# Shift and scale in units of four k-tiles, their column sums by transposes, in a hybrid decoder layer

## The chip, the cores and the metric

The kernel runs on one core of a Trainium2 chip. The metric is the device time of one execution in microseconds; a lower time is better. TensorE (PE) multiplies matrices, VectorE (DVE) and ScalarE (ACT) work on tiles, SyncE (SP) issues all transfers from HBM; each engine runs its own queue in order, and waits on semaphores for the others.

## What is computed

One decoder layer for 256 tokens of width 4096, in fp32. The part that matters here is the adaptive norm ahead of the first projection:

```python
c_act = jax.nn.silu(c)
mod = c_act @ w_ada[l] + b_ada[l]              # (1, 4096) @ (4096, 3 * 4096)
shift, scale, gate = jnp.split(mod, 3, axis=-1)
h = rmsnorm(x, norm_gain[l])
h = h * (1.0 + scale[:, None, :]) + shift[:, None, :]
proj = jnp.einsum('bsd,dn->bsn', h, w_in[l])   # (256, 4096) @ (4096, 12288)
```

Behind it come sixteen attention heads and four pooling groups on the 24 blocks of 512 columns of `proj`, their gating, the product with `w_out` (4096 x 4096), the factor `gate` with the residual, and a last rmsnorm.

## The kernel before

**Products.** The width of 4096 is cut into 32 k-tiles of 128. `proj` is cut into 24 chunks of 512 columns, which `order` lists. Each fp32 operand is split into a rounded high part and the rest; a product takes three matmuls of 512 columns (high x high, high x low, low x high), for two row tiles of tokens. `split_piece` brings two k-tiles of one chunk (512 KB into a `raw` tile, 7 buffers), lets ACT cast them to `wh` (L237) and DVE take the difference `wl` (L238), 3 buffers each; `products` (L248) issues the 12 matmuls: eight on `wh`, then four on `wl`.

**Visits.** The activations `h` of a k-tile exist only once its shift and scale are summed over all 4096 rows of `w_ada`. The kernel doesn't wait for all of them. It goes round the 24 chunks again and again (L372 to L381), and each `visit` multiplies the chunk by the k-tiles that have become ready since its last visit, in an accumulator `mm` (2 buffers). A chunk's first visit ends with a copy by ACT (L289), each later one with an addition to `accs` by DVE (L291), which here is called its eviction.

**Units.** Shift and scale are made in units of k-tiles (`UNITS`, two each, sixteen in all). `ada_tasks` cuts a unit into tasks of one `raw` tile: 1024 columns of fp32, which are two row blocks of `w_ada` times 2 x 256 columns, in two transfers of 256 KB with rows of 1 KB. `ada_acc` multiplies each block by its column of silu(c) and adds it to `aacc` (128 x 512) with one DVE instruction (L161; the first is L159). `ada_hook` runs after every piece: it adds `2 * RATES[built]` to a credit and runs one task for every 1.456 (`ADA_COST`) of it. With the last task of a unit `build_h` sums `aacc` over its 128 partitions, adds bias and gain (`s12`), and makes the high and low parts `hh` and `hl` of `h` for its k-tiles (ACT L221 and L223, DVE L224). The unit counts as ready two hooks later (`LAG`). The first unit is made ahead of all visits. When all 32 k-tiles are ready the last round of visits runs, with the attention and pooling work, the gate's own additions (`gacc`) and `w_out` behind it.

**Order.** The instructions of each engine stand in an order that the framework's scheduler has fixed when the kernel is built; a tile's number in an order below tells its instance.

In `build_h` before, the sum over partitions is a matmul of each block with a column of ones:

```python
for j in range(2 * uk):
    nc.tensor.matmul(pc[:, j:j + 1], lhsT=acc[:, j * P:(j + 1) * P], rhs=ones, start=True, stop=True)
```

## Time and profile before

| | us |
|---|---|
| median of 3 runs (1558.37 to 1562.53) | 1560.77 |
| profiled execution | 1562.59 |
| its span, first to last instruction | 1560.8 |
| PE busy (7043 instructions) | 1513.5 (97%) |
| DVE busy (1766) | 1409.9 (90%) |
| ACT busy (830) | 703.6 (45%) |

The kernel moves 491 MB, at a mean of 315 GB/s. A matmul that is busy need not be at its peak, since matmuls overlap; the distance from one start to the next is the better measure. Times in the rows are counted from the span's start.

### The profile page before, as it was taken

What the parts mean: (1) busy time and instruction counts of PE and PEld (TensorE: products, weight loads), DVE (VectorE), ACT (ScalarE), POOL (GpSimd) and SP (SyncE); (2) the same over time, 40 slices, a digit from 0 to 9 for tenths busy, and PEclk for the clock granted to TensorE, in tenths of its full rate; (3) what the DMA queues carried; (4) which work ended last, traced back from release to release, by engine and by line L of the source; (5) the groups of instructions that cost most, each with busy time, mean ns of one, the idle gap of its engine ahead of it and who ended that gap; (6) DMA issues with size and microseconds to landing.
All of it is one profiled execution on the core that took longest, in us unless ns stands there. A gap on an engine that the chain in (4) does not pass through costs nothing.

```text
span 1560.8 us, 20366 instructions
## 1 busy us (share of the span) xinstructions
PE 1513.5 (97%) x7043; PEld 1259.0 (81%) x7043; DVE 1409.9 (90%) x1766; ACT 703.6 (45%) x830; POOL 0.7 (0%) x5
## 2 busy tenths in 40 slices
PE   2999999999999999999999999999999999999997
PEld 2877888888888888888888888888898888888875
DVE  5888999999999999899999998999988889988886
ACT  5655343443443434344344344566654444444444
POOL 0000000000000000000000000000000000000000
PEclk9999999999999999999999999999999999999999
DMA  9999999999999999999999998977678999998886
GB/s 330 348 337 356 320 330 324 321 314 338 319 318 328 309 330 310 309 314 328 350 342 324 332 330 305 319 259 231 212 247 269 308 329 358 348 321 325 324 313 258
DMA packets 324087, 491.11 MB, mean 315 GB/s; under 512 B 19320, under 2 KB 150664, under 8 KB 323984
## 3 DMA queue, kind: packets, MB, share of 16 engines
q1 hardware_dynamic: 323984, 489.82, 92.6%
q8 instruction: 55, 0.90, 0.2%
q14 instruction: 48, 0.39, 0.1%
HBM read 485.55 MB, written 4.19 MB: 314 GB/s over the span
## 4 chain that ended last, share of the span: by engine, by line
PE 88%; DVE 4%; DMA 4%; issue 2%; ACT 1%; SPq 1%; DVEq 0%; ACTq 0%
PE mm L248 80%; DMA raw<-in_w_ada_dram 3%; DVE aacc L161 2%; DVE wl L238 1%; PE psm L618 1%; PE psm L248 1%; PE psm L208 1%; PE psm L524 0%; PE psm L523 0%; PE psm L522 0%; DMA raw<-in_w_in_dram 0%; DMA sb<-in_x_dram 0%; PE psm L435 0%; DMA raw<-in_w_out_dram 0%; ACT wh L237 0%
## 5 line engine op out<-in xcount | busy, mean ns | idle before, releaser
L237 ACT CAST wh<-raw 128x1024 fp32r<-128x1024 f32 x514 | 538.4, 1050 | 688.4 <-PE mm L248 547.4
L238 DVE TENSOR_TENSOR wl<-raw,wh 128x1024 fp32r<-128x1024 f32 x514 | 624.5, 1218 | 33.6 <-ACT wh L237 31.6
L248 PE MATMUL mm<-wh,hh 128*128 128x512 f32 x1536 | 604.4, 393 | 5.4 <-ACT wh L237 4.3
L248 PE MATMUL mm<-wh,hl 128*128 128x512 f32 x1536 | 600.1, 391 | 0.0
L248 PE MATMUL mm<-wl,hh 128*128 128x512 f32 x1536 | 414.2, 391 | 0.7 <-DVE wl L238 0.6
L161 DVE SCALAR_TENSOR_TENSOR aacc<-raw,cact,aacc 128x512 f32<-128x512 f32 x496 | 370.9, 748 | 30.2 <-DMA raw<-in_w_ada_dram 22.7
L248 PEld LDWEIGHTS mm<-wh,hh 128*128 128x128 f32 x1536 | 288.8, 188 | 66.8 <-ACT wh L237 7.3
L248 PEld LDWEIGHTS mm<-wl,hh 128*128 128x128 f32 x1536 | 288.4, 188 | 61.3 <-DVE wl L238 1.6
L248 PEld LDWEIGHTS mm<-wh,hl 128*128 128x128 f32 x1536 | 288.9, 188 | 58.2
L248 PE MATMUL mm<-wh,sa 128*128 128x512 f32 x896 | 221.7, 389 | 0.0
L161 DVE SCALAR_TENSOR_TENSOR gacc<-raw,cact,gacc 128x512 f32<-128x512 f32 x248 | 185.6, 748 | 24.9 <-DMA raw<-in_w_ada_dram 21.2
L248 PEld LDWEIGHTS mm<-wh,sa 128*128 128x128 f32 x896 | 168.0, 188 | 34.9
L248 PE MATMUL mm<-wl,sa 128*128 128x512 f32 x448 | 119.8, 389 | 0.0
L291 DVE TENSOR_TENSOR sa<-mm,sa 128x1024 f32<-128x1024 f32 x92 | 112.1, 1218 | 8.6 <-PE mm L248 8.4
L248 PEld LDWEIGHTS mm<-wl,sa 128*128 128x128 f32 x448 | 84.0, 188 | 17.6 <-DVE wl L238 0.2
L291 DVE TENSOR_TENSOR sb<-mm,sb 128x1024 f32<-128x1024 f32 x48 | 58.5, 1219 | 7.3 <-PE mm L248 7.3
L328 PE MATMUL psm<-diag_r,sb 128*128 128x128 f32 x128 | 17.8, 310 | 15.6 <-DVE diag_r L320 15.6
L328 PEld LDWEIGHTS psm<-diag_r,sb 128*128 128x128 f32 x128 | 17.5, 225 | 15.8 <-DVE diag_r L320 15.8
L221 ACT ACTIVATE hf<-xT,s 128x256 f32<-128x256 f32 x32 | 17.5, 594 | 26.0 <-DVE s L213 26.0
L289 ACT COPY sa<-mm 128x1024 f32<-128x1024 f32 x16 | 16.3, 1016 | 15.1 <-PE mm L248 15.1
L672 ACT ACTIVATE yo<-sb 128x512 f32<-128x512 f32 x16 | 10.0, 626 | 25.0 <-DVE sb L670 25.0
L248 PE MATMUL psm<-wh,sa 128*128 128x512 f32 x80 | 20.1, 393 | 0.6 <-ACT wh L237 0.6
(118 smaller groups left out, 632.7 us busy)
## 6 DMA issues: line engine op xcount, KB each, us to landing
raw<-in_w_in_dram SPq DMA_DIRECT2D x384, 512.0 KB, 5.6
raw<-in_w_ada_dram SPq DMA_DIRECT2D x512, 256.0 KB, 5.4
raw<-in_w_ada_dram SPq DMA_DIRECT2D x128, 512.0 KB, 6.0
raw<-in_w_out_dram SPq DMA_DIRECT2D x128, 512.0 KB, 6.4
sb<-in_x_dram SPq DMA_DIRECT2D x16, 512.0 KB, 6.0
raw<-in_w_pool_dram SPq DMA_DIRECT2D x8, 512.0 KB, 4.4
out_dram<-sb SPq DMA_DIRECT2D x16, 256.0 KB, 2.6
fg<-in_final_gain_dram SPq DMA_DIRECT2D x8, 256.0 KB, 4.7
```

Of the source, the lines that this page charges most:

```text
L161: nc.vector.scalar_tensor_tensor(out=acc, in0=r, scalar=cact[:, kt:kt + 1], in1=init if kt == 0 else acc, op0=ALU.mult, op1=ALU.add)
L208: nc.tensor.matmul(pc[:, j:j + 1], lhsT=acc[:, j * P:(j + 1) * P], rhs=ones, start=True, stop=True)
L221: nc.scalar.activation(out=hf[:, i], in_=xT[:, kk + i], func=AF.Identity, scale=s12[:, 1, a + i:a + i + 1], bias=s12[:, 0, a + i:a + i + 1])
L237: nc.scalar.copy(out=wh[:, 0:n], in_=v[:, 0:n])
L238: nc.vector.tensor_tensor(out=wl[:, 0:n], in0=v[:, 0:n], in1=wh[:, 0:n].bitcast(F32), op=ALU.subtract)
L248: nc.tensor.matmul(pt[t], lhsT=hv[i][p][:, t * P:(t + 1) * P], rhs=w[:, i], start=started, stop=ended)
L289: nc.scalar.copy(out=accs[ch], in_=pt)
L291: nc.vector.tensor_tensor(out=accs[ch], in0=pt, in1=accs[ch], op=ALU.add)
L328: nc.tensor.matmul(px[:, i * S + t * P:i * S + (t + 1) * P], lhsT=xs[q][:, t, (2 * a + i) * P:(2 * a + i + 1) * P], rhs=diag_r[:, t], star ...
L618: nc.tensor.matmul(pt[t], lhsT=h[:, t * P:(t + 1) * P], rhs=w, start=False, stop=last and e == len(seq) - 1)
L672: nc.scalar.activation(out=y[:, t], in_=xc[:, t], func=AF.Square, accum_out=ss2[:, t, n:n + 1])
```

## The change

From the third unit on a unit has four k-tiles: `UNITS` is (2, 2, 4, 4, 4, 4, 4, 4, 4). A `raw` tile then holds one row block times 2 x 512 columns, one transfer of 512 KB with rows of 2 KB, and one DVE instruction adds 1024 columns. A unit of four has 32 tasks, one of two has 16; the tasks are 240 behind the first unit in both. In `build_h` the column of ones is gone: each 128 x 128 block of `aacc` is transposed by PE, four to a bank, and DVE adds the four blocks along their rows with one `tensor_reduce`. RATES falls from 0.8 to 0.72 while the third unit is made and rises from 0.5, 0.46 and 0.5 to 0.52 in the three behind it.

```diff
-UNITS = (2,) * 16
+UNITS = (2, 2) + (4,) * 7
-RATES = (0.8, 0.8, 0.8, 0.5, 0.46, 0.5, 0.5, 0.5, 0.48, 0.5, 0.5, 0.54)
+RATES = (0.8, 0.8, 0.72, 0.52, 0.52, 0.52, 0.5, 0.5, 0.48, 0.5, 0.5, 0.54)
-    ones = const.tile([P, 1], F32, name="ones")
-    nc.vector.memset(ones, 1.0)
-                    acc.append(pool.tile([P, 2 * HB * P], F32, name="aacc")[:, 0:w])
+                    acc.append(pool.tile([P, 2 * max(UNITS) * P], F32, name="aacc")[:, 0:w])
-        pc = misc()
-        for j in range(2 * uk):
-            nc.tensor.matmul(pc[:, j:j + 1], lhsT=acc[:, j * P:(j + 1) * P], rhs=ones, start=True, stop=True)
-        s12 = const.tile([P, 2, HB], F32, name="s12", bufs=2)
+        pc = const.tile([P, 2 * max(UNITS)], F32, name="pc", bufs=2)
+        for j0 in range(0, 2 * uk, 4):
+            pt = misc()
+            for j in range(4):
+                nc.tensor.transpose(out=pt[:, j * P:(j + 1) * P], in_=acc[:, (j0 + j) * P:(j0 + j + 1) * P],
+                                    identity=ident)
+            nc.vector.tensor_reduce(out=pc[:, j0:j0 + 4], in_=pt.rearrange("p (j d) -> p j d", d=P),
+                                    axis=AX.X, op=ALU.add)
+        s12 = const.tile([P, 2, max(UNITS)], F32, name="s12", bufs=2)
```

Since the sizes of the units set which k-tiles a visit finds ready, the visits change too. Ahead of the last round there are 140 in before and 160 in after. In before, builds stand on PE behind 14, 29 and 52 pieces, and so on; in after behind 14, 47, 91, 136, 181, 227, 274 and 323. Lines have other numbers in after: L238 is L241, L248 is L251, L291 is L294, L224 is L227, L161 is L159 and L159 is L157.

DVE in before, at the start of the second round of visits (`wl` is a difference, `aacc` a scaled addition, `sa` and `sb` evictions of `accs`):

```order
L238 TENSOR_TENSOR wl_1260<-raw_1257,wh_1259 128x1024
L291 TENSOR_TENSOR sa_385<-mm_1208,sa_385 128x1024
L238 TENSOR_TENSOR wl_1278<-raw_1275,wh_1277 128x1024
L161 SCALAR_TENSOR_TENSOR aacc_1158<-raw_1293,cact_74,aacc_1158 128x512 x2
L238 TENSOR_TENSOR wl_1303<-raw_1300,wh_1302 128x1024
L291 TENSOR_TENSOR sa_411<-mm_1256,sa_411 128x1024
L161 SCALAR_TENSOR_TENSOR aacc_1158<-raw_1318,cact_74,aacc_1158 128x512
L238 TENSOR_TENSOR wl_1326<-raw_1323,wh_1325 128x1024
```

DVE in after, at the same place:

```order
L241 TENSOR_TENSOR wl_1162<-raw_1159,wh_1161 128x1024
L159 SCALAR_TENSOR_TENSOR aacc_769<-raw_1177,cact_74,aacc_769 128x1024
L294 TENSOR_TENSOR sa_385<-mm_1158,sa_385 128x1024
L241 TENSOR_TENSOR wl_1185<-raw_1182,wh_1184 128x1024
L159 SCALAR_TENSOR_TENSOR aacc_769<-raw_1200,cact_74,aacc_769 128x1024
L294 TENSOR_TENSOR sa_411<-mm_1181,sa_411 128x1024
L241 TENSOR_TENSOR wl_1208<-raw_1205,wh_1207 128x1024
L159 SCALAR_TENSOR_TENSOR aacc_769<-raw_1223,cact_74,aacc_769 128x1024
L294 TENSOR_TENSOR sb_437<-mm_1204,sb_437 128x1024
```

In before two differences stand between two evictions, in after one; this goes on for the sixteen chunks whose second visit covers one piece.

DVE in before, at the build of the third unit, behind 29 pieces (`psm_1124` holds PE's column sums, `s12` shift and scale, `hl` the low part of `h`):

```order
L211 TENSOR_TENSOR s12_1129<-psm_1124,colB_72 128x2
L212 TENSOR_TENSOR s12_1129<-psm_1124,colA_71 128x2
L238 TENSOR_TENSOR wl_1143<-raw_1140,wh_1142 128x1024
L213 TENSOR_TENSOR s12_1129<-s12_1129,gb_76 128x2
L159 TENSOR_SCALAR aacc_1158<-raw_1159,cact_74 128x512
L161 SCALAR_TENSOR_TENSOR aacc_1158<-raw_1159,cact_74,aacc_1158 128x512
L238 TENSOR_TENSOR wl_1168<-raw_1165,wh_1167 128x1024
L224 TENSOR_TENSOR hl_1134<-hf_1135,hh_1133 128x512
```

DVE in after, at the build of the third unit, behind 47 pieces:

```order
L210 TENSOR_REDUCE pc_1480<-psm_1481 128x4
L210 TENSOR_REDUCE pc_1480<-psm_1487 128x4
L214 TENSOR_TENSOR s12_1493<-pc_1480,colB_72 128x4
L294 TENSOR_TENSOR sb_772<-mm_1512,sb_772 128x1024
L215 TENSOR_TENSOR s12_1493<-pc_1480,colA_71 128x4
L241 TENSOR_TENSOR wl_1536<-raw_1533,wh_1535 128x1024
L216 TENSOR_TENSOR s12_1493<-s12_1493,gb_75 128x4
L241 TENSOR_TENSOR wl_1559<-raw_1556,wh_1558 128x1024
L294 TENSOR_TENSOR sb_796<-mm_1532,sb_796 128x1024
L157 TENSOR_SCALAR aacc_1551<-raw_1552,cact_74 128x1024
L241 TENSOR_TENSOR wl_1580<-raw_1577,wh_1579 128x1024
L227 TENSOR_TENSOR hl_1498<-hf_1499,hh_1497 128x512
```

The two reductions are new, and evictions now stand between the sums and `hl`.

PE in after, behind the transposes of that build (`wh_1535` is piece 48, `wh_1558` piece 49):

```order
L251 MATMUL mm_1532<-wh_1535,hl_742 128x512
L251 MATMUL mm_1532<-wl_1536,hh_741 128x512 x4
L251 MATMUL mm_1555<-wh_1558,hh_1497 128x512
L251 MATMUL mm_1596<-wh_1599,hh_1497 128x512
L251 MATMUL mm_1555<-wh_1558,hl_1498 128x512
```

The second piece behind the build reads the tiles that the build makes; in before the new tiles `hh_739` are read by the first piece behind its build at this place.

## Rows read from the trace of the kernel before

**Rows 1.** The page: busy us (share of the span) and instructions, by engine.
```profile
PE 1513.5 (97%) x7043; PEld 1259.0 (81%) x7043; DVE 1409.9 (90%) x1766; ACT 703.6 (45%) x830; POOL 0.7 (0%) x5
```

**Rows 2.** Chain of waits in order of time, 330 to 600: start, us, what.
```profile
334.29 0.79 PE psm L208 x8
335.08 62.69 PE mm L248 x276
```

**Rows 3.** Timeline of PE at groups of L208: start, us, operation, tiles, count.
```profile
48.94 0.47 PE L248 MATMUL mm<-wh,hh 128*128 128x512 f32 x1
...
91.12 0.95 PE L208 MATMUL psm<-ones,aacc 128*128 128x1 f32 x8
...
201.73 0.95 PE L208 MATMUL psm<-ones,aacc 128*128 128x1 f32 x8
...
202.86 0.40 PE L248 MATMUL mm<-wh,hl 128*128 128x512 f32 x1
...
956.60 0.95 PE L208 MATMUL psm<-ones,aacc 128*128 128x1 f32 x8
```

**Rows 4.** PE's waits, 49 to 202 us: us in total, times, longest.
```profile
PE mm L248 <- ACT wh L237: 4.3, 4, 2.0
```

**Rows 5.** Timeline of DVE, 151 to 158 us: start, us, operation.
```profile
152.29 1.22 DVE L291 TENSOR_TENSOR sa<-mm,sa 128x1024 f32<-128x1024 f32 x1
153.43 1.22 DVE L238 TENSOR_TENSOR wl<-raw,wh 128x1024 fp32r<-128x1024 f32 x1
154.56 1.53 DVE L161 SCALAR_TENSOR_TENSOR aacc<-raw,cact,aacc 128x512 f32<-128x512 f32 x2
156.01 1.22 DVE L238 TENSOR_TENSOR wl<-raw,wh 128x1024 fp32r<-128x1024 f32 x1
```

**Rows 6.** Groups of DVE by form: count, busy us, mean ns, idle before.
```profile
L238 DVE TENSOR_TENSOR wl<-raw,wh 128x1024 fp32r<-128x1024 f32 x514 | 624.5, 1218 | 33.6 <-ACT wh L237 31.6
L161 DVE SCALAR_TENSOR_TENSOR aacc<-raw,cact,aacc 128x512 f32<-128x512 f32 x496 | 370.9, 748 | 30.2 <-DMA raw<-in_w_ada_dram 22.7
L224 DVE TENSOR_TENSOR hl<-hf,hh 128x512 fp32r<-128x512 f32 x16 | 10.9, 684 | 0.0
L159 DVE TENSOR_SCALAR aacc<-raw,cact 128x512 f32<-128x512 f32 x16 | 7.7, 480 | 4.6 <-DMA raw<-in_w_ada_dram 4.6
L442 DVE TENSOR_REDUCE st<-sm 128x1 f32<-128x256 f32 x16 | 6.5, 408 | 0.0
L442 DVE TENSOR_REDUCE st<-sm 128x1 f32<-128x128 f32 x16 | 4.4, 277 | 0.0
```

**Rows 7.** Stretches: busy us by engine, granted PE clock, DMA share, GB/s.
```profile
80.00:90.00 10.00, 8.81 (x32) 7.12 (x33) 7.70 (x9) 5.56 (x7) 0.00 (x0) 0.83 1.07 366
115.00:145.00 30.00, 28.51 (x126) 22.40 (x125) 26.01 (x34) 17.00 (x19) 0.00 (x0) 1.00 1.07 366
300.00:350.00 50.00, 50.00 (x226) 41.54 (x225) 47.52 (x56) 20.43 (x21) 0.00 (x0) 1.00 0.96 318
1450.00:1500.00 50.00, 50.00 (x222) 41.37 (x221) 45.28 (x51) 21.79 (x25) 0.00 (x0) 1.00 0.93 338
```

**Rows 8.** Timeline of PE at four transposes, 982 to 986 us.
```profile
983.00 0.60 PE L411 MATMUL psm<-ident,sa 128*128 128x128 f32 x4
...
983.66 0.40 PE L248 MATMUL mm<-wh,hl 128*128 128x512 f32 x1
```

**Rows 9.** Timeline of PE behind its longest wait; in brackets idle before, releaser.
```profile
81.19 0.50 PE L248 MATMUL mm<-wh,hh 128*128 128x512 f32 x1 [2.05 <-ACT wh L237]
...
83.51 1.91 PE L248 MATMUL mm<-wl,hh 128*128 128x512 f32 x4
...
87.48 1.07 PE L248 MATMUL mm<-wl,hh 128*128 128x512 f32 x4
```

**Rows 10.** Groups of ACT: count, busy us, mean ns, idle before.
```profile
L221 ACT ACTIVATE hf<-xT,s 128x256 f32<-128x256 f32 x32 | 17.5, 594 | 26.0 <-DVE s L213 26.0
...
L223 ACT CAST hh<-hf 128x512 fp32r<-128x512 f32 x16 | 9.9, 618 | 0.2
```

## Prediction

> **What bounds the kernel now.** I read the page first: TensorE (PE) is busy 97% of the span [rows 1]. The chain of waits in order of time then shows what fills it: unbroken runs of product matmuls, broken only by the column sums of L208 [rows 2]. I call a *piece* what one call of `split_piece` brings: two k-tiles of one chunk, 512 KB, one cast on ACT, one difference on VectorE (DVE), 12 matmuls. 276 matmuls are 23 pieces in 62.69 us, 2.72 us each. The starts of the L208 groups on PE [rows 3] say where PE loses time. The order of instructions puts 14 pieces ahead of the second group and 52 ahead of the fourth (201.73 us). One group costs 0.90 us: 201.73 to the second matmul behind it at 202.86, less one matmul spacing of 0.23. From 201.73 to 956.60 lie 273 pieces and 12 groups: 742.6 + 10.8 = 753.4 of 754.9 us. So after 201 us PE is the bound and nothing else is late there. Before that it loses: 91.12 - 48.94 = 42.2 for 14 pieces (38.1), 4.1 lost; 201.73 - 91.12 = 110.6 for 38 pieces and two groups (103.4 + 1.8), 5.4 lost. PE's waits in that stretch are for the cast [rows 4]. A change to this kernel can therefore gain in three places alone: PE's own small work, the 9.5 us lost before 201 us, and a tail that it does not touch.
>
> **Fewer builds, cheaper on PE.** From 201 us on, before has 13 groups of four L208 sums, 13 x 0.90 = 11.7 us on the path. After has six groups of eight transposes there (behind 91, 136, 181, 227, 274 and 323 pieces). Four transposes cost 0.43 us at L411 (983.00 to 983.66, less 0.23), a further one 0.11 [rows 8], so eight cost 0.87: 6 x 0.87 = 5.2. **Gain 6.5 us.** Is a later build hidden otherwise? Take T as the end of its transposes. DVE then reduces twice (a reduction of 128 takes 0.277, of 256 0.408, so 512 about 0.67 [rows 6]), and between the three short additions the order puts one difference and one scaled addition, so s12 is ready at T + 4.2. ACT has two casts ahead of `hf` in its queue; then come three `hf`, a cast and the fourth `hf` (0.55 to 0.62 each [rows 10]), 2.8 us, and the next `wh` at T + 8.2. PE has four pieces to run until T + 10.9. I cost the wait at nothing; its cover is 2.7 us. The new tiles are first read at least three pieces later.
>
> **DVE's work.** A scaled addition of 512 takes 0.748; from 512 to 1024 a tensor_tensor grows by 1.218 - 0.684 = 0.534 [rows 6], so 1024 columns take 1.28 where two took 1.50. Back to back, a difference or an eviction starts the next instruction 1.14 later and a pair of additions 1.45 later [rows 5]; the wide one I put at 1.21. Between two later builds the order holds 45 differences, 19 evictions and 32 additions, 73 + 39 + 3 for the build = 115 us against 45 x 2.72 + 0.87 = 123 of PE. DVE is relieved there, and worth nothing: PE is the bound. SP issues one transfer of 512 KB for two of 256; also nothing, since PE waits for no issue after 201 us.
>
> **The start is where it costs.** The first 14 pieces are alike in both (4.1 lost again). The second build moves nothing. The third comes after 47 pieces and no longer after 29, and is twice as large.
>
> *Pieces 15 to 32.* One weight piece and one ada tile a piece, 1.05 MB in 2.72 us = 385 GB/s. In this stretch before moved 366 GB/s, its engines busy all the time (share 1.07) [rows 7]. At 366 a piece takes 2.86, so 18 pieces lose 2.6. But a stage whose rows are 2 KB throughout moves 338 at a share of 0.93 (363 per full share), the mixed stage 318 at 0.96 (331) [rows 7]: the same engines would move 366 x 363 / 331 = 401, and lose nothing. I take 0.8, and 0.7 for the cast that stands behind `hf` at the second build, as in before: **1.5 lost** (0.7 to 3.3).
> The Trainium skill ("DMA: Bandwidth & Descriptors", Specifications) gives full line rate from 512 bytes on, by which longer rows gain nothing here; the two shares above speak against it. By that rule this stretch loses 3.3 and the time below would be 1568.
>
> *Pieces 33 to 47.* Here is the main cost. Units one and two are ready, so the second round of visits runs from k-tile 2 to 4: one piece a visit, and each visit ends in an eviction on DVE. In before the same visits run from 2 to 6, two pieces to one eviction, and RATES has already fallen to 0.5. After, the rate stays at 0.72 (an addition nearly every piece). DVE's order is then difference, addition, eviction, 1.14 + 1.21 + 1.14 = 3.49 us a piece, against 2.72 on PE. The eviction of piece 33 cannot start before that piece ends, so there is no lead to spend. From there to the eviction of piece 46 the order holds 14 differences, 13 additions, 13 evictions: 46.5 us. PE can be one piece ahead (two accumulators), and ends piece 47 at about 46.3, the transposes at T = 47.5.
> Then the drain: DVE reduces (to 49.0), evicts, and only then makes `wl` of piece 48 (51.6). PE, done with its `wh` products at 49.3, waits 2.3 and ends the piece at 52.5. Piece 49 needs the new tiles. s12 is ready at 51.7, `hh` at 54.0, but `hl` stands on DVE behind a difference, an eviction, the first product of the next unit (0.48 for 512, some 0.75 for 1024 [rows 6]) and another difference: 56.6. PE has two matmuls to run meanwhile, so piece 49 starts in effect at 56.1. Fifteen pieces and the transposes are 41.7: **14.4 lost** (8 if DVE's spacings overlap better, 18 if every handover costs 0.2 more).
> Behind that DVE has slack again and PE runs on.
>
> *Clock.* Before lost 2.05 us once, and 1.5 us later eight matmuls ran at twice the spacing (four took 1.91 where four take 1.07) [rows 9]; the granted clock of that stretch is 0.83 [rows 7], part of it 1.2 GHz instead of 2.4. That is 1.6 us. After has two such waits close together: **1.6 more** (0 to 3.2).
>
> **The sum.** Start: 4.1 + 1.5 + 14.4 + 1.6 lost and 0.43 + 0.87 for two builds, 22.9, against 9.5 + 1.8 = 11.3 before: +11.6. Later builds: -6.5. Together +5.1. The profiled execution has a span of 1560.8 and took 1562.59, so 1567.7 on its own scale; it lies 1.8 above the median 1560.77. **Forecast: 1566 us**, slower by 0.3%, which is about what a measurement of this kernel can tell from no change. Own range of this case: 1561 to 1571.
>
> **Rivals.**
> *1. DVE keeps up in the start (1554).* Place: pieces 33 to 47. If difference, addition and eviction came every 2.75 us or less and the drain hid behind pieces already cast, the start would lose what it lost before, and only the 6.5 us of the later builds would be left. The change breaks even once the stretch and drain lose 9.3 and not 14.4, a cycle of 3.1 us. For it: DVE was busy 47.5 of 50 us in the steady stage [rows 7], with an order that sums to about PE's pace, and PE lost nothing. Against it: the spacings of [rows 5] are measured back to back, and no cover is in the queue. 0.2.
> *2. The long rows do not speed up the transfers (1568).* By the 366 GB/s of [rows 7]. 0.1.
> *3. Every later build stalls PE (1574).* The chain of 8.2 us under a cover of 10.9 fails if s12 comes 4 us later, for instance because DVE waits for PE at the reductions with the differences queued behind them; 6 x 1.3 us. Against it: 0.79 at each group and nothing more in before [rows 2]. 0.08.
> *4. The clock falls through the whole stretch (1578).* At half clock a piece takes 12 x 0.43 = 5.2 us, 1.7 more than DVE's cycle; over half of the 14 pieces that is 12 us. For it: PE pauses in each piece there. Against it: the one fall in before followed a wait of 2.05 us [rows 9], these are under 0.8. 0.07.
> The Trainium skill ("TensorE: Matmul & The Clock Gate", A second HAM failure mode) tells of a kernel whose short pauses between accumulator groups made the clock swing, which is this case; no row here shows it.
> *5. Half of it is covered (1561).* The drain costs half and the transfers are quick. 0.1.
>
> **How the numbers follow.** Forecast 0.45, half of it below +0.3%, half above. Faster by over 0.3%: most of rival 1, 0.17. Within 0.3%: half the forecast, rival 5 and the rest of rival 1, 0.35. Slower: the other half and rivals 2 to 4, 0.48. The range runs from the low end of rival 1 to rival 3: 1554 to 1575.
>
> **What would show it.** Right: the profile of after gives DVE, in a stretch of about 50 us that begins near 145 us, busy without a break in triples of difference, addition and eviction, PE at some 175 matmuls in it and not 226; two PE waits of 2 to 4 us near 195 us; the fourth group of transposes 0.9 us long with no wait behind it; and from there 45 pieces and 0.87 us from group to group, 123.4 us. Wrong: the wide addition well off 1.28 us, PE waiting for `wl` or `hl` behind the later groups, or a granted clock under 1 between 150 and 200 us.

## Result and profile after

The changed kernel takes 1576.7 us (median of 4 runs, 1572.5 to 1577.1) against 1559.6 us of the kernel before beside it: 1.0101 times as long, 95% interval 1.0078 to 1.0124. It is slower, as forecast, but by 17 us and not by 5, and 1.7 us outside the range. The profiled execution took 1576.69 us, its span is 1574.9.

The page of after, busy us by engine (as in [rows 1]):

```profile
PE 1516.5 (96%) x6979; PEld 1250.0 (79%) x6979; DVE 1400.0 (89%) x1556; ACT 702.4 (45%) x830; POOL 0.7 (0%) x5
```

DVE has 10 us less to do than before, and the kernel is longer. Where the time went is again read from the starts of the groups of L208 on PE (timeline of PE, as [rows 3]: start, us, operation, tiles, count):

```profile
90.02 0.60 PE L208 MATMUL psm<-ident,aacc 128*128 128x128 f32 x4
...
190.13 1.09 PE L208 MATMUL psm<-ident,aacc 128*128 128x128 f32 x8
...
318.43 1.03 PE L208 MATMUL psm<-ident,aacc 128*128 128x128 f32 x8
...
441.74 1.03 PE L208 MATMUL psm<-ident,aacc 128*128 128x128 f32 x8
...
691.07 1.03 PE L208 MATMUL psm<-ident,aacc 128*128 128x128 f32 x8
...
824.46 1.03 PE L208 MATMUL psm<-ident,aacc 128*128 128x128 f32 x8
...
964.34 1.03 PE L208 MATMUL psm<-ident,aacc 128*128 128x128 f32 x8
```

From 318.43 to 441.74 are 45 pieces and one group: (123.31 - 0.87) / 45 = 2.721 us a piece, nothing lost. I use 2.721 and 0.87 (0.43 for a group of four, 0.90 for the column sums of before) from here on; *lost* is the time from one group to the next beyond them. The order puts the groups behind 14, 47, 91, 136, 181, 227, 274 and 323 pieces. From 691.07 to 824.46 are 47 pieces: 4.6 us lost. From 824.46 to 964.34 are 49: 5.7 lost. The forecast had nothing there.

The waits in that stretch, 692 to 950 us (engine, line, tile, what it waited for, us in total, times, longest):

```profile
DVE aacc L159 <- DMA raw<-in_w_ada_dram: 34.7, 36, 2.2
...
PE mm L251 <- DVE sb L294: 2.1, 2, 1.3
PE mm L251 <- DVE wl L241: 1.8, 4, 0.8
```

The same line from 320 to 690 us, where nothing is lost:

```profile
DVE aacc L159 <- DMA raw<-in_w_ada_dram: 8.5, 13, 1.1
```

So PE waits for evictions and differences, and DVE in its turn for ada tiles: 34.7 us in 258, against 8.5 in 370. The waits of PE that the profile names in the two stretches add up to 6.3 of the 10.3 us lost; the rest is in gaps and spacings that it puts down to nothing. One such stall, first in the timeline of DVE (start, us, operation; in brackets the idle time before and its releaser):

```profile
750.81 1.21 DVE L241 TENSOR_TENSOR wl<-raw,wh 128x1024 fp32r<-128x1024 f32 x1
751.94 1.28 DVE L159 SCALAR_TENSOR_TENSOR aacc<-raw,cact,aacc 128x1024 f32<-128x1024 f32 x1
753.14 2.35 DVE L241 TENSOR_TENSOR wl<-raw,wh 128x1024 fp32r<-128x1024 f32 x2
756.95 1.28 DVE L159 SCALAR_TENSOR_TENSOR aacc<-raw,cact,aacc 128x1024 f32<-128x1024 f32 x1 [1.46 <-DMA raw<-in_w_ada_dram]
758.15 1.22 DVE L241 TENSOR_TENSOR wl<-raw,wh 128x1024 fp32r<-128x1024 f32 x1
760.17 1.28 DVE L159 SCALAR_TENSOR_TENSOR aacc<-raw,cact,aacc 128x1024 f32<-128x1024 f32 x1 [0.80 <-DMA raw<-in_w_ada_dram]
761.37 1.22 DVE L294 TENSOR_TENSOR sb<-mm,sb 128x1024 f32<-128x1024 f32 x1
```

then in that of SP, which issues the ada tiles,

```profile
752.05 0.37 SPq L190 DMA_DIRECT2D raw<-in_w_ada_dram  x1
...
754.38 0.37 SPq L190 DMA_DIRECT2D raw<-in_w_ada_dram  x1
```

and in that of PE:

```profile
762.73 0.47 PE L251 MATMUL mm<-wh,hh 128*128 128x512 f32 x1 [1.29 <-DVE sb L294]
```

The difference that starts at 750.81 is the last reader of a raw buffer. SP issues the next ada tile into that buffer at 752.05, as soon as the difference is done. In DVE's order only one addition and two differences, 3.5 us of work, stand between that difference and the addition that reads the new tile. A transfer of 512 KB takes 5.2 to 5.6 us from issue to landing (medians of the DMA view). So DVE stands idle for 1.46 us, at the next tile for 0.80, the eviction behind them starts late, and PE, which needs that accumulator, waits 1.29.

I call these 3.5 us the **lead** of an addition: the DVE work that the order of instructions puts between the one that frees a raw buffer and the scaled addition that reads the tile loaded into it. I counted it for each kernel from its order of instructions, with 1.14 us for a difference or an eviction, 1.21 and 0.73 for a wide and a narrow addition, 0.6 for a reduction (rows of the traces). I call a lead *short* if it is under 5 us, less than a transfer takes. From group to group in after, of 32 additions none, none, 3, 12, 30 and 30 have a short lead; the last two stretches are those that lose 4.6 and 5.7 us. Their median lead is 4.6 us, that of the first is 8.1.

### The profile page after: what moved, and what is told of

It is laid out like the page before. It is cut to its first block, busy times and chain, and to the rows that moved or that the text cites. A ratio compares the mean times of both kernels' runs of the same rounds, so it can differ in the third digit from the quotient of the medians.

```text
span 1574.9 us, 19748 instructions
## 1 busy us (share of the span) xinstructions
PE 1516.5 (96%) x6979; PEld 1250.0 (79%) x6979; DVE 1400.0 (89%) x1556; ACT 702.4 (45%) x830; POOL 0.7 (0%) x5
## 4 chain that ended last, share of the span: by engine, by line
PE 79%; DMA 9%; DVE 7%; issue 3%; SPq 0%; ACT 0%; DVEq 0%; ACTq 0%
PE mm L251 70%; DMA raw<-in_w_ada_dram 8%; DVE wl L241 4%; DVE aacc L159 1%; PE psm L621 1%; DVE sa L294 1%; PE psm L251 1%; PE psm L331 1%; DVE sb L294 1%; DMA sb<-in_x_dram 1%; PE psm L527 0%; PE psm L526 0%; PE psm L525 0%; PE psm L414 0%; PE psm L438 0%
## 5 line engine op out<-in xcount | busy, mean ns | idle before, releaser
L241 DVE TENSOR_TENSOR wl<-raw,wh 128x1024 fp32r<-128x1024 f32 x514 | 621.8, 1218 | 36.5 <-ACT wh L240 34.3
L251 PE MATMUL mm<-wh,hh 128*128 128x512 f32 x1536 | 605.9, 395 | 10.4 <-ACT hh L226 3.0
L251 PE MATMUL mm<-wh,hl 128*128 128x512 f32 x1536 | 600.9, 391 | 0.8 <-DVE hl L227 0.8
L251 PE MATMUL mm<-wl,hh 128*128 128x512 f32 x1536 | 417.0, 393 | 7.4 <-DVE wl L241 7.3
L159 DVE SCALAR_TENSOR_TENSOR aacc<-raw,cact,aacc 128x1024 f32<-128x1024 f32 (+1 forms) x279 | 324.2, 1162 | 54.5 <-DMA raw<-in_w_ada_dram 52.6
L251 PEld LDWEIGHTS mm<-wh,hh 128*128 128x128 f32 x1536 | 289.3, 188 | 76.0 <-ACT wh L240 8.3
L251 PEld LDWEIGHTS mm<-wl,hh 128*128 128x128 f32 x1536 | 287.6, 188 | 73.7 <-DVE wl L241 14.7
L251 PEld LDWEIGHTS mm<-wh,hl 128*128 128x128 f32 x1536 | 289.3, 188 | 60.2 <-DVE hl L227 1.8
L251 PE MATMUL mm<-wh,sa 128*128 128x512 f32 x896 | 221.6, 389 | 0.0
L159 DVE SCALAR_TENSOR_TENSOR gacc<-raw,cact,gacc 128x512 f32<-128x512 f32 x248 | 185.6, 748 | 29.0 <-DMA raw<-in_w_ada_dram 25.1
L251 PEld LDWEIGHTS mm<-wh,sa 128*128 128x128 f32 x896 | 167.9, 188 | 35.0 <-ACT wh L240 0.3
L294 DVE TENSOR_TENSOR sa<-mm,sa 128x1024 f32<-128x1024 f32 x104 | 126.7, 1219 | 12.0 <-PE mm L251 10.4
L251 PE MATMUL mm<-wl,sa 128*128 128x512 f32 x448 | 119.8, 389 | 0.0
L251 PEld LDWEIGHTS mm<-wl,sa 128*128 128x128 f32 x448 | 84.1, 188 | 17.5
L294 DVE TENSOR_TENSOR sb<-mm,sb 128x1024 f32<-128x1024 f32 x56 | 68.3, 1219 | 5.9 <-PE mm L251 4.7
L224 ACT ACTIVATE hf<-xT,s 128x256 f32<-128x256 f32 x32 | 17.5, 594 | 11.3 <-DVE s L216 11.3
L251 PE MATMUL psm<-wh,sa 128*128 128x512 f32 x80 | 19.9, 391 | 1.4 <-ACT wh L240 1.4
```

The lines of the kernel that those rows point to most:

```text
L159: nc.vector.scalar_tensor_tensor(out=acc, in0=r, scalar=cact[:, kt:kt + 1], in1=init if kt == 0 else acc, op0=ALU.mult, op1=ALU.add)
L224: nc.scalar.activation(out=hf[:, i], in_=xT[:, kk + i], func=AF.Identity, scale=s12[:, 1, a + i:a + i + 1], bias=s12[:, 0, a + i:a + i + 1])
L241: nc.vector.tensor_tensor(out=wl[:, 0:n], in0=v[:, 0:n], in1=wh[:, 0:n].bitcast(F32), op=ALU.subtract)
L251: nc.tensor.matmul(pt[t], lhsT=hv[i][p][:, t * P:(t + 1) * P], rhs=w[:, i], start=started, stop=ended)
L294: nc.vector.tensor_tensor(out=accs[ch], in0=pt, in1=accs[ch], op=ALU.add)
```

## Experiments

All times are medians beside runs of the kernel before on the same chip (1560.6 to 1561.4); "ratio" is to these. Where nothing else is said, an edit is one to the changed kernel.

**Another rate late in the stream.**

```diff
-RATES = (0.8, 0.8, 0.72, 0.52, 0.52, 0.52, 0.5, 0.5, 0.48, 0.5, 0.5, 0.54)
+RATES = (0.8, 0.8, 0.72, 0.52, 0.52, 0.52, 0.52, 0.52, 0.52)
```

> The changed kernel with one edit: the last entries of RATES are 0.52 instead of 0.50, 0.50, 0.48, so that the order of pieces and ada tiles of the lossless stretch (318 to 691 us) goes on to the end of the stream. Theory A (the 10.4 us that PE loses between 691 and 964 us come from the order in which ada tiles and weight tiles take the seven raw buffers): they go, 1576.7 - 10.4 = about 1566 us, and PE starts its transposes every 123.3 us to the end. Rival B (that part of the stream is slow for wide tiles whatever the order, by the transfers or by larger visits): the time stays at 1573 to 1577. Rival C (more ada tiles per piece only make it worse, DVE being the bound): over 1578.

Measured: 1567.3 us, ratio 1.0048 (1.0034 to 1.0061). The groups follow each other in 123.3 us (120.6 for 44 pieces) from the fourth to the last; the loss is gone. DVE's waits between 692 and 950 us, the first line for the cast, the second for ada tiles:

```profile
DVE wl L241 <- ACT wh L240: 15.1, 27, 1.3
...
DVE aacc L159 <- DMA raw<-in_w_ada_dram: 1.9, 5, 0.8
```

Theory A holds, C falls: more additions to a piece, and less waiting. Short leads are 4, 5 and 7 of 32 in the last three stretches, where after has 12, 30 and 30. Behind the stream the profiled execution (1571.2 us, the slowest of the five) takes 5.4 us more than before for the same pieces.

**Units of four only from the fifth on.**

```diff
-UNITS = (2, 2) + (4,) * 7
+UNITS = (2,) * 4 + (4,) * 6
-RATES = (0.8, 0.8, 0.72, 0.52, 0.52, 0.52, 0.5, 0.5, 0.48, 0.5, 0.5, 0.54)
+RATES = (0.8, 0.8, 0.8, 0.5, 0.52, 0.52, 0.52, 0.52, 0.52, 0.52)
```

> The changed kernel with units three and four of two k-tiles again and the rate 0.8 of the kernel before for the third (so the first 52 pieces and three builds are ordered as in the kernel before), units of four only from the fifth on, and 0.52 for all later ones as in the run with that edit alone. Theory (the one-piece visits with a scaled addition each, and the drain behind the third build, cost the start 11 to 12 us): it is 11 to 12 us below the run with the late rates alone, 1554 to 1555 if that is 1566. Rival (the large unit costs the same wherever the first one stands, since the order then holds 25 evictions and 32 wide additions in 44 pieces): the loss moves behind piece 52 and the two runs are within 3 us.

Measured: 1580.8 us, ratio 1.0134 (1.0120 to 1.0148): the worst of the variants that compute the same. Both theories were too simple. The start is that of before again (the fourth group at 197.53 us, before 201.73). But behind it 5.4, 13.7, 9.1 and 0.8 us are lost. The first of these is the stretch with one-piece visits, where DVE's work (120.4 us by the order) is as long as PE's. Of the 13.7, 9.9 are lost in the first two pieces behind the build that ends it: PE waits for `hh`, and the granted clock is 0.50 from 324 to 337 us (timeline of PE).

```profile
330.65 1.22 PE L251 MATMUL mm<-wh,hh 128*128 128x512 f32 x2 [5.80 <-ACT hh L226]
```

So the loss of the start belongs to the first large unit and moves with it, as the rival had it. The other 3.8 and the 9.1 lie where 28 and 27 of 32 leads are short, with 29 us of DVE's waits for ada tiles; in the next two stretches, 0.8 and 0 lost, it is 11 each.

**The transposes alone, in the kernel before.** The changed kernel with `UNITS = (2,) * 16` and the rates of before.

> The kernel before (units of two k-tiles, its rates) with the column sums made by transposes and one reduction, nothing else. Theory (a later build is hidden but for PE's own time): each of 15 groups takes 0.43 us of PE instead of 0.90, so 6 to 7 us less than the kernel before, about 1553. Rival (the reduction of 512 columns, 0.67 us on DVE in every build, and the longer way to s12 make PE wait): no gain, 1558 to 1562.

Measured: 1563.9 us, ratio 1.0023 (1.0011 to 1.0035); it is not the 6 us faster that the cheaper groups would make it. The term itself is right: at most groups 0.45 us are saved (63.48 becomes 63.03, 66.20 becomes 65.78). But between 525 and 721 us 9.9 us are lost (1.7, 4.0, 4.2 in three groups), and 3.7 more behind the stream. The waits there:

```profile
DVE aacc L159 <- DMA raw<-in_w_ada_dram: 16.4, 18, 3.2
...
PE mm L251 <- DVE sa L294: 5.3, 3, 2.3
```

It is the late loss of after again, in a kernel with no wide addition and no ada tile with rows of 2 KB. Behind the longest of these waits of PE the granted clock is 0.50 from 666 to 669 us, which makes 1.7 of the last 4.2. The order has 18 short leads among the 64 additions of these three groups and the one ahead of them, and none behind. The kernel before has 10 at the same pieces, and loses 1.3 us. That PE has 0.47 us less to do at each group and DVE a reduction of 0.68 more, and so less slack to catch up, is my reading of the difference and was not tested by itself.

**Eight raw buffers.** Eight to the end of the kernel could not be timed: they do not fit into the memory on the chip (one pool needs 34 KB per partition, 31.7 are left). So there is one more slot in the stream, one buffer of sums fewer, and behind the stream the buffers are seven again in a pool of their own.

```diff
-    adap = ada_cm.enter_context(tc.tile_pool(name="ada", bufs=2, side="right"))
+    adap = ada_cm.enter_context(tc.tile_pool(name="ada", bufs=1, side="right"))
+    rawp.append(ada_cm.enter_context(tc.tile_pool(name="raws", bufs=RAWB + 1, side="right")))
...
-        return strm.tile([P, RAW], F32, name="raw", bufs=RAWB)
+        return rawp[-1].tile([P, RAW], F32, name="raw")
...
     ada_cm.close()
+    rawp.append(ctx.enter_context(tc.tile_pool(name="rawl", bufs=RAWB)))
```

> The changed kernel with eight raw buffers in the stream of blocks instead of seven (its room comes from one buffer of sums instead of two; behind the stream the buffers are seven again, in a pool of their own). Theory A (late in the stream a transfer is issued too late because its buffer comes free too late): with 14% more room every transfer goes out 1.6 us earlier, the 4.5 and 5.5 us lost from the seventh and the eighth group of transposes on go, 1566. If the start is set by DVE's own work, the 100.1 and 128.3 us from the second and the third group stay within 1 us. Rival B (the DMA engines are the limit there): 4.5 and 5.5 us stay, 1575 to 1578.

Measured: 1572.1 us, ratio 1.0070 (1.0056 to 1.0084). In the stream theory A holds: 128.75 and 134.18 us in place of 133.39 and 139.88, nothing lost; DVE's waits for ada tiles are not among the waits of that stretch any more (short leads: 0, 1 and 1 of 32). The start is unmoved (100.12 and 128.03 us), so it is not the buffers that set it. The 6 us that the total lacks lie behind the stream: where the pool changes PE waits once for 4.1 us, and the work there takes 7.2 us more than in before. That this is the price of my edit is likely for the 4.1 us and not shown for the rest, since runs without a change of pools lose as much there (below).

The same with small units:

> The kernel before with transposes (units of two k-tiles) and eight raw buffers in the stream. With seven it lost 9.7 us between 525 and 721 us and gained 0.45 us at each other group. Theory A (that loss too is a matter of when raw buffers come free): it goes, and the groups follow each other in 2.72 us a piece and 0.43 to the end, 1554, 6 us under the kernel before. Rival B (transfers or DVE are the limit): 1562 to 1565 again.

Measured: 1559.5 us, ratio 0.9993 (0.9984 to 1.0002). Nothing lost from the fourth group to the last, which starts at 945.69 us, 10.9 before that of the kernel before [rows 3]; 11.0 us are given back behind the stream, with the change of pools, so the expected 1554 is missed.

**Half of the transfers, half of the additions.** In the first the tile's second half is not loaded and the first is read twice; in the second only 512 columns are added. Both so compute other shifts and scales.

```diff
-                    nc.sync.dma_start(out=v[:, 0], in_=wa_v[:, kts[0], 0:2, cs])
+                    nc.sync.dma_start(out=v[:, 0, 0:1], in_=wa_v[:, kts[0], 0:1, cs])
...
+            if len(kts) == 1:
+                r = rt[:, 0:width // 2].unsqueeze(1).to_broadcast([P, 2, width // 2])
+                acc = acc3
```

```diff
+            if len(kts) == 1 and kt > 0:
+                r, acc = rt[:, 0:width // 2], acc[:, 0:width // 2]
```

> The changed kernel with half of each ada tile of a large unit left out of the transfer (256 KB instead of 512 KB); the scaled addition still has 1024 columns, and reads the half that came twice. The output is that of other shifts and scales. It keeps DVE's work and takes a fifth of the stream's bytes away. Theory A (DVE's own work sets the start, transfers issued late set the late loss, since a shorter transfer lands earlier): the time from the third group of transposes to the fourth stays near 128 us, the late 10 us go: 1564 to 1567. Rival B (the start is set by the transfers too): 128 falls to 122 and the 100.1 ahead of it to 92, 1550 to 1555. Rival C (DVE's work alone sets both): 1575 to 1577.

Measured: 1595.5 us, ratio 1.0223 (1.0207 to 1.0240), outside every theory: with fewer bytes the kernel is the slowest of all. The experiment is not the clean one that I took it for. Its order is another one: some 200 of DVE's 1524 instructions stand elsewhere (the fewest that have to move to turn one order into the other), the additions late in the stream nearer to their transfers. The median lead is 3.4 us, the shorter transfers land in 3.6 (median), and each of the five later stretches loses 4.7 to 8.8 us. DVE's waits from 310 to 985 us:

```profile
DVE aacc L163 <- DMA raw<-in_w_ada_dram: 84.9, 89, 2.3
```

DMA engines are busy 78 to 80% there, at 242 to 251 GB/s, against 95 to 98% in after between 340 and 650 us, where it loses nothing. So a busy DMA is not the cause. The place of the additions is what is left; no run changes it back alone.

The start shrinks too, which matters for the account below: the stretch ahead of the third group takes 93.7 us and not 100.1, about what rival B had, though every addition is whole; the next stays at 128.0, as in theory A. DVE sits idle for 1.8 us in pieces 15 to 32 where it does for 5.4 in after, and has 20 additions behind it there instead of 18.

> The changed kernel with the scaled additions of a large unit on 512 of the 1024 columns (0.75 us instead of 1.28), the first of each unit whole; all transfers as they are. The output is that of other shifts and scales. Theory A (DVE's own work sets the start and its lack of slack lets a late tile through to TensorE): the stretch from the second group to the third falls from 100.1 to about 92 to 93 (15 pieces with 0.5 us less each), 128.3 to 124, and the late 10 us go or fall by more than half: 1553 to 1558. Rival B (the transfers set both): 1574 to 1577. Rival C (DVE sets the start, the transfers set the late loss): 1563 to 1567.

Measured: 1558.6 us, ratio 0.9981 (0.9971 to 0.9990), within what theory A expected. This order is another one too (200 instructions moved), and the third group stands behind 46 pieces, not 47. So the first two stretches (94.3 us for 32 pieces, 124.9 for 45) can be held against after only together: 8.4 us lost where after loses 17.6. Late it is 128.75 and 135.00 us, 0 and 0.8 lost. In the first of these only 6 of 32 leads are short. In the last, 812 to 946 us, 26 are, and DVE waits longer than in after (20.2 us from 824 to 964):

```profile
DVE aacc L161 <- DMA raw<-in_w_ada_dram: 31.2, 21, 3.6
```

Yet PE loses 0.8. So short leads alone need not cost PE anything. With 0.5 us less for each addition DVE is busy 101 of 134 us there, and 121 of 140 in after; that this slack makes the waits good is my reading.

**The lead chosen from the order, then measured.** Small units with transposes, the rates from the fourth on changed to one value:

```diff
-RATES = (0.8, 0.8, 0.8, 0.5, 0.46, 0.5, 0.5, 0.5, 0.48, 0.5, 0.5, 0.54)
+RATES = (0.8, 0.8, 0.8) + (0.52,) * 13
```

> The kernel with units of two k-tiles and transposes again, with one edit: every rate from the fourth on is 0.52. I call the lead of a scaled addition the DVE work that the order puts between the instruction that frees a raw buffer and the addition that reads the tile loaded into it (1.14 us a difference or eviction, 0.73 and 1.21 a narrow or wide addition). A transfer takes 5.2 to 5.6 us from issue to landing, so a lead under that makes DVE wait, with the next differences and evictions queued behind. In the run with 0.46 to 0.50 the lead fell to 5.6 us (median) in the stretch that lost 9.7 us, and stood at 7 to 9 elsewhere. Here it is 8.6 from end to end. Theory (lead): nothing is lost from the fourth group on, 1560.6 less 2.8 (the start, as measured there) less 12 x 0.47 = 1552. Rival (DVE's total work: more additions per piece leave DVE no slack): over 1560, with differences late in many places.

> The same with every rate from the fourth on at 0.50: the same instructions, fewer additions to a piece, so more slack on DVE, but the median lead falls to 6.0 us at piece 190, 5.6 at 240 and 4.3 to 4.9 from 265 to 330. Theory (lead): the groups behind piece 190 lose 1 to 4 us each, 1565 to 1575, and DVE waits for ada tiles there. Rival (DVE's total work): as fast as the run at 0.52 or faster, 1550 to 1554.

Measured: 1559.8 us at 0.52, ratio 0.9990 (0.9979 to 1.0002), and 1575.9 at 0.50, ratio 1.0095 (1.0074 to 1.0115). At 0.52 the stream loses nothing, as expected, but the work behind it takes 6 us more than in before, so the total misses the expected 1552. PE's first wait there, 930 to 1557 us:

```profile
PE psm L455 <- DVE sm L448: 4.8, 3, 2.8
```

At 0.50 the last three groups, with 10, 13 and 15 short leads of 16, lose 1.7, 8.3 and 0.4 us; those with 2 to 5, at medians of 5.6 to 6.9, lose nothing, which I had expected to cost already. DVE's wait there, between 770 and 910 us:

```profile
DVE aacc L159 <- DMA raw<-in_w_ada_dram: 16.3, 16, 2.4
```

The run with less DVE work per piece is the slower one by 16 us, 10.4 of them lost in its last three groups (1.6 of these by a granted clock of 0.50 behind a wait of PE of 2.1 us) and 5 behind the stream. That rules DVE's total work out as the cause of this loss.

The same test on large units, and the search for a version better than both. The three runs have four, six and eight small units ahead of the large ones, with 0.54, 0.54 and 0.53 late in the stream:

> The run with four small units and six large ones (1580.8 us, 28 us lost behind the fourth group) with 0.54 in place of 0.52 for the large ones. There the median lead was 4.6 us from piece 98 to 187, here it is 8 to 10. Theory (lead): the 13.5, 9.0 and 0.7 us lost behind the fifth, sixth and seventh group go; what is left is the stretch from piece 52 on with its one-piece visits, where DVE's work is as long as TensorE's (5 us lost): 1557 to 1559. Rival (the large units cost DVE what they cost there): 1575 or more.

Measured: 1568.3 us, ratio 1.0045 (1.0033 to 1.0057), 12.5 us under the run at 0.52. The expected 1557 to 1559 are missed. No lead is short, and the losses of 13.7, 9.1 and 0.8 shrink to 6.0, 0 and 0. All of the 6.0 come in the first three pieces behind the build that ends the one-piece visits, where DVE's work (114.7 us) is again as long as PE's (115.1): PE waits 1.7 us for `wl` and 3.2 for `hh`, and the granted clock is 0.50 from 326 to 332 us. So what the short leads cost at 0.52, 3.8, 9.1 and 0.8, is gone, and the drain is left. Another 6 us come behind the stream.

> The changed kernel with six small units ahead of five large ones and 0.54 for all units from the fifth on. Lead 7 us or more throughout, three visits of one piece behind the first large unit instead of ten, and DVE's work by the order 112 us against 118 of TensorE in the first stretch with large units. Theory (lead, and one-piece visits for the start): no loss from the fourth group on, 1560.6 - 2.8 - 0.47 x 3 for the small groups, and 0.93 less for each of five large ones: about 1551 to 1553. Rival (the large unit always costs a stall of its own): 1557 or more.

Measured: 1557.0 us, ratio 0.9974 (0.9965 to 0.9983): faster than both kernels, 4 us under before and 20 under after, though not the 1551 to 1553 expected. In its stream 5.1 us are lost, in pieces of about 1. What waits is no longer DVE for ada tiles but the cast for weight tiles (196 to 908 us):

```profile
ACT wh L240 <- DMA raw<-in_w_in_dram: 287.1, 166, 4.3
```

At 0.54 the additions come so early that, as I read it, the seven buffers hold ada tiles, and the weight tiles come late instead. With small units at 0.52 the same line has 63.1 us.

> Eight small units, four large ones, rates 0.52 up to the eighth unit and 0.53 behind. The lead by the order is 7 us or more throughout and no stretch has more DVE work than TensorE work. Theory (lead): nothing lost from the fourth group to the last, 4.5 us less there than the run with six small units (1557.0), so 1552 to 1553 if the work behind the stream takes what it took there, and up to 1558 if it loses the 6 us that it lost in the run with 0.52 and small units alone. Rival: the 4.5 us are the price of large units, and come again: 1557 or more with losses at the large groups.

Measured: 1560.4 us, ratio 0.9995 (0.9985 to 1.0005). The stream loses 1.4 us from the fourth group on, against 5.1, as the lead theory says; behind it 6 us are lost. The total lies 2.4 us above the upper end of what I had expected (1558).

| run | stretch, in pieces | short leads | lost, us |
|---|---|---|---|
| after | 136 to 181; 181 to 227 | 3 and 12 of 32 | 0; 0 |
| after | 227 to 274; 274 to 323 | 30 and 30 of 32 | 4.6; 5.7 |
| late rate 0.52 | 226 to 270; 270 to 315 | 5 and 7 of 32 | 0; 0 |
| eight buffers | 227 to 274; 274 to 323 | 1 and 1 of 32 | 0; 0 |
| half of the transfers, which land in 3.6 us | 227 to 274; 274 to 323 | 30 and 31 of 32 | 7.3; 4.7 |
| half of the additions | 274 to 323 | 26 of 32 | 0.8 |
| four small units, 0.52 | 96 to 140; 140 to 185; 185 to 230; 230 to 275 | 28, 27, 11 and 11 of 32 | 13.7 (9.9 of them the drain); 9.1; 0.8; 0 |
| small units, 0.50 | 261 to 284; 284 to 308; 308 to 331 | 10, 13 and 15 of 16 | 1.7; 8.3; 0.4 |
| small units, 0.52 | 51 to 319 | 0 of 192 | 0 |
| transposes in before | 171 to 194; 194 to 218; 218 to 239 | 7, 5 and 2 of 16 | 1.7; 4.0; 4.2 |
| transposes, eight buffers | the same three | 1, 3 and 2 of 16 | 0; 0; 0 |

The count tells where time can be lost, not how much: in the rows of small units the loss does not follow it, and in half of the additions nearly all leads are short and almost nothing is lost.

**What stays open.** The work behind the stream, which no edit touches, takes about as long as in before for the same pieces in some runs (after 1.0 more, six small units none, four small units at 0.52 0.8 less) and 2 to 12 us more in the others. Part of it is seen: with small units at 0.52, PE waits there 4.8 us in three places for DVE's score tiles of the attention heads (`sm`), a wait that before does not have; with the late rate 0.52 it is 4.0 us, with four small units at 0.54 4.4, with eight 3.2. What sets it was not tried. Nor is it settled why the scheduler moves additions toward their transfers. It does so at a lower rate (0.50 against 0.52 with small units, and late in after), but with four small units also at 0.52.

## Why the prediction was right and wrong

**The start was right, in size and place.** Lost time ahead of the fourth group and in the drain was to grow by 12.1 us (4.1 + 1.5 + 14.4 + 1.6 against 9.5). From the first group to 318.43 us after loses 27.1 us, before in the same pieces 14.7: 12.4 more. The total is closer than its parts, since the first two below miss by 1.3 and 1.5 us in opposite directions.

- Pieces 15 to 32, forecast 1.5: 0.2. Their transfers ran at 387 GB/s (first line below, columns as in [rows 7]; [rows 7] had 366), so rival 2 falls.
- Pieces 33 to 47, forecast 8.2 to the end of piece 47: 9.7. DVE goes without a break in triples, one every 3.65 us (forecast 3.49), and PE makes 180 matmuls in 50 us where [rows 7] has 226. With 512 columns added instead of 1024 the start (pieces 15 to 91) loses 8.4 us instead of 17.6, so DVE's work sets it, as forecast. It does not do so alone: with half of the bytes, and every addition whole, it loses 10.9. There DVE runs ahead in pieces 15 to 32, which, as I read it, after's order and its full DMA engines (share 1.05) did not let it; the forecast's main term took only the spacing from piece 33 on. Both runs have another order, and neither parts the two by itself.
- The drain and the clock, forecast 6.2 + 1.6: 7.7.

Stretches of after:

```profile
112.00:138.00 26.00, 26.00 (x116) 21.55 (x115) 22.56 (x20) 14.66 (x15) 0.00 (x0) 1.00 1.05 387
140.00:190.00 50.00, 45.15 (x180) 31.93 (x178) 47.91 (x42) 17.42 (x17) 0.00 (x0) 1.00 0.91 300
200.00:210.00 10.00, 10.00 (x36) 8.08 (x37) 7.98 (x8) 3.15 (x3) 0.00 (x0) 0.80 0.82 277
```

A triple on DVE and the start of the next, timeline from 149 us:

```profile
149.84 1.23 DVE L294 TENSOR_TENSOR sb<-mm,sb 128x1024 f32<-128x1024 f32 x1
150.98 1.22 DVE L241 TENSOR_TENSOR wl<-raw,wh 128x1024 fp32r<-128x1024 f32 x1
152.12 1.28 DVE L159 SCALAR_TENSOR_TENSOR aacc<-raw,cact,aacc 128x1024 f32<-128x1024 f32 x1
153.49 1.22 DVE L294 TENSOR_TENSOR sb<-mm,sb 128x1024 f32<-128x1024 f32 x1
```

PE in the drain, timeline from 194 us; the last row is at half the clock, 1.2 GHz instead of 2.4 (four of these take 1.07 us in [rows 9]):

```profile
194.87 1.20 PE L251 MATMUL mm<-wl,hh 128*128 128x512 f32 x4 [1.42 <-DVE wl L241]
197.99 1.22 PE L251 MATMUL mm<-wh,hh 128*128 128x512 f32 x2 [1.92 <-ACT hh L226]
199.78 0.80 PE L251 MATMUL mm<-wh,hl 128*128 128x512 f32 x1 [0.57 <-DVE hl L227]
...
202.93 1.61 PE L251 MATMUL mm<-wl,hh 128*128 128x512 f32 x4
```

**The later builds were right in size**: a group costs 0.9 us (45 and 46 pieces with one group take 123.31 and 126.03 us), no wait of `hf` or `hh` behind it reaches PE, and six of them for thirteen are the 6.5 us forecast. Wide addition 1.28 us, reduction 0.68, first product 0.74: all as taken.

**The step that failed** is the one on DVE's work behind the start: "DVE is relieved there, and worth nothing: PE is the bound", and behind it, of the transfers, "also nothing, since PE waits for no issue after 201 us". It took the steady state of before for that of after. The term costed at nothing measured 10.3 us, and 1.0 came behind the stream. In spans the forecast was 1565.9 us (1560.8 + 5.1) and after has 1574.9, 9.0 more: these 11.3 and 0.3 of the start, less 1.3 that before loses in its own stream and after does not, and less 1.3 at and ahead of the first group, which no term of the forecast has. The medians are 10.7 apart because the profiled execution of before lay 1.8 above its median.

In after the loss is made by the new order, in which nearly all leads are short over the last 96 pieces of the stream. But the trace of before has it in small, and the prediction read past it: of the 754.9 us from 201.73 to 956.60 its sum left 1.5 unexplained, and 1.3 of them are lost between 659.69 and 719.00. There DVE's addition waits for its ada tile, the eviction behind it comes late, and PE waits (before, two rows of DVE, then one of PE):

```profile
662.44 0.75 DVE L161 SCALAR_TENSOR_TENSOR aacc<-raw,cact,aacc 128x512 f32<-128x512 f32 x1 [2.50 <-DMA raw<-in_w_ada_dram]
663.11 1.22 DVE L291 TENSOR_TENSOR sa<-mm,sa 128x1024 f32<-128x1024 f32 x1
664.47 0.47 PE L248 MATMUL mm<-wh,hh 128*128 128x512 f32 x1 [0.99 <-DVE sa L291]
```

The check that would have caught it was open: the changed order can be read, and the landing time of a transfer is in the page of before (5.4 to 5.6 us). Summing DVE's work over a stretch (115 us against 123) was not enough, since both sums stay the same while the addition moves toward its transfer.

**Rivals.** 1 falls with the start. 2 falls with the 387 GB/s. The Trainium skill ("DMA: Bandwidth & Descriptors", Specifications) gives full line rate from 512 bytes on. The rows do not agree: a stretch whose ada tiles have rows of 2 KB, one transfer each, moved 387 GB/s, one with rows of 1 KB in two transfers 366, both with all engines busy (shares 1.05 and 1.07); whether the rows or the transfers make the difference is not shown. 3 and 4 named times near the measured one (1574 and 1578) by other mechanisms. 3 falls: no later build of after stalls PE for `hf` or `hh`. 4 falls: the granted clock is 1.00 from 140 to 190 us although PE pauses in each piece; behind that it fell once in the start, in the second of the two waits of the drain (0.80 from 200 to 210 us, matmuls 0.43 us apart for 0.23 until 204 us). The Trainium skill ("TensorE: Matmul & The Clock Gate", A second HAM failure mode) tells of a clock that swings with short pauses between accumulator groups. That swing is not seen here. 5 falls.

Two of the signs of being wrong came: PE waits for `wl` late in the stream (1.8 us, four times), and the granted clock is under 1 before 200 us (0.86 from 190 to 200), which the drain's clock term had priced.

The likeliest case was right and incomplete. The range was too narrow on the slow side, since no rival had a wait between transfers and their readers in the steady state.

## What to carry to other kernels

Where a few buffers are shared by two streams and an engine consumes both in a fixed order, measure in the new order how much work stands between the instruction that frees a buffer and the one that reads what is loaded into it, and hold it against the landing time of a transfer; sums of work over a stretch do not show it. How much of such a wait gets through is another matter: 34.7 us of them went with some 10 lost on PE in after, 31.2 with 0.8 where each addition was half as wide. A rate that feeds one stream later can starve it, a rate that feeds it earlier can starve the other: here 0.50 made additions wait for their tiles, 0.54 made casts wait for theirs, and 0.52 lost nothing in two orders but not in a third (four small units). So the order has to be read each time.

## What the runs showed of the hardware

- Fewer bytes went with a kernel slower by 19 us (half of the transfers, 1595.5 against 1576.7), in an order with shorter leads, with DMA engines 78 to 80% busy.
- Rows of 2 KB alone, in transfers of 512 KB, moved 387 GB/s (share 1.05) where 1 KB and 2 KB mixed, in transfers of 256 and 512 KB, moved 366 (share 1.07, [rows 7]).
- In after two waits of PE of 1.42 and 1.92 us within 4.6 us went with a granted clock of 0.50 from 198 to 204 us; ten matmuls ran 0.43 to 0.44 us apart instead of 0.23, 2 us in all. Single waits of 2.31 and 2.13 us (transposes in before, small units at 0.50) were each followed by 0.50 for some 3 us, which cost 1.7 and 1.6. Pauses of at most 0.6 us in each piece, over 50 us, went with a clock of 1.00.
